# Score matmuls in fours, x scaled in one VectorE pass, and another order of the seven products

## The chip, the cores and the metric

The kernel runs on one core of a Trainium2 chip. Its engines are TensorE (PE in the profile; PEld are its weight loads), VectorE (DVE), ScalarE (ACT), GpSimd (POOL) and SyncE (SP, which here issues most of the DMA transfers). Each engine works through its own queue in order, and semaphores tie the queues together. The metric is the device time of one execution in microseconds (us); lower is better. The kernel before took 2226.36 us, the median of 3 runs (2225.69 to 2230.63).

## What is computed

One layer of a streaming encoder, for a prompt of 512 tokens and for 8 running streams with 16 new tokens each, 640 tokens in all, of width 2048. One input projection feeds 6 stick-breaking heads, 6 band heads and 4 memory heads of width 128, their gates, and three merge gates of width 2048:

```python
def rms_norm(x, g):
    xf = x.astype(jnp.float32)
    xf = xf * lax.rsqrt(jnp.mean(xf * xf, axis=-1, keepdims=True) + RMS_EPS)
    return (xf * g.astype(jnp.float32)).astype(x.dtype)

def stick_breaking(q, k, v, q_pos, k_pos):
    z = jnp.einsum('bqhd,bkhd->bhqk', q, k).astype(jnp.float32) * (HEAD_DIM ** -0.5)
    ...

def merge_output(x, o_sb, g_sb, o_bd, g_bd, o_mm, g_mm, mg_sb, mg_bd, mg_mm,
                 w_up_sb, w_up_band, w_up_mem, w_out, g_post):
    ...
    merged = (jax.nn.sigmoid(mg_sb) * branch(o_sb, g_sb, w_up_sb)
              + jax.nn.sigmoid(mg_bd) * branch(o_bd, g_bd, w_up_band)
              + jax.nn.sigmoid(mg_mm) * branch(o_mm, g_mm, w_up_mem))
    return x + rms_norm(merged @ w_out, g_post)
```

Three places matter here. `rms_norm(x, g_pre)` is applied to x before the projection. The scores q·k of the sample tokens against the cached keys of each stream (512 keys, 256 in the memory heads) stand in all three kinds of attention. The merge gates are sigmoids of the columns of `rms_norm(x) @ w_in` that belong to them.

## The kernel before

**Numbers and tiles.** Activations lie transposed, channels on the 128 partitions and the 640 tokens in two halves of 320 (`HF`). A projection multiplies in three matmuls: each weight and each activation is split into a high and a low part (`split`, L96 on ACT for the high part, L97 on DVE for the low), and high by high, high by low and low by high are added up (`mm3`, L148 to L150, and `proj`, L162). Weights come in pieces: SP loads a tile `wr`, ACT and DVE make `wh` and `wl` of it, 128x512 at a time, with four buffers each, and PE uses them.

**Stages.** From 0 to 97 us the keys and values of the memory tokens are projected (L148 to L150 into `acc`), and woven into that the five tiles of x are loaded, normalised, transposed on PE and split (`norm_x`, L232 to L249): ACT sums the squares (L185), DVE works out the scale (`rms_scale`, L131 to L137, on 128x1 tiles `rs`), POOL multiplies by the gain `gbx` (L237), DVE by the scale (L238), PE transposes (L243). Until 985 us follow the twelve causal heads, alternately stick-breaking and band; until 1190 us the four memory heads and the first four gates; until about 1742 us the other 44 gates as 22 pairs; then the upward projections and the output projection with its norm.

**A head.** Four projections give gate, value, query and key. Then `interleave` takes turns between the attention of the prompt and `sample_att`. The latter handles the eight streams in two rounds (`par` 0 and 1) of four. For each stream, DVE transposes cached keys `kc` into a tile `kt` (L486, four buffers); then four matmuls (L490) multiply 32 columns of `qm` each by one `kt` and write 32 partitions each of the score tile `s`, at column position 32·j of the array.

**A pair of gates.** `gate_pair` computes two column blocks by two halves of the tokens with seven products in place of eight. Each `product` is 24 matmuls (L687) into one of three banks `qa`, `qb`, `qc`; products on `qa` accumulate through the pair, and after some of them the bank is copied (ACT) or added (DVE, L697) into the output tiles `o0`, `o1`, on which ACT then applies the sigmoid. The weight sums s1 to s4 are made on POOL.

**Order.** The code is written with tiles and dependencies; a scheduler of the tile framework sets, when the program is built, the order of every engine's queue, by a timeline of its own. `tc.issue_after` limits where an instruction may stand in the queue and adds no wait.

Of the kernel before, what the change touches and what calls it, by code (L numbers as in the profile page):

```python
# [11 lines left out]
ALU = mybir.AluOpType  # L12
# [31 lines left out]
def stream_step_kernel(  # L44
# [8 lines left out]
    PE, ACT, DVE, POOL, SP = nc.tensor, nc.scalar, nc.vector, nc.gpsimd, nc.sync  # L53
# [122 lines left out]
    with ExitStack() as m0:  # L176
# [27 lines left out]
        for k0 in range(0, KB, 2):  # L204
            tp = bank("tp").rearrange("p (k n) -> p k n", k=2)
            for kk in range(2):
                k = k0 + kk
                for t in range(2):
# [4 lines left out]
                                         op0=ALU.mult, op1=ALU.subtract)  # L213
# [11 lines left out]
        gbx = pm.tile([P, D], F32, name="gbx")  # L225
# [6 lines left out]
        def norm_x(t):  # L232
            xr = raw_rows()
            for v, src in blocks(xr, x_p, x_s, t):
                SP.dma_start(v, src)
            r = rms_scale(sumsq(xr), pm, "rs0")
            POOL.tensor_tensor(xr, xr, gbx, op=ALU.mult)  # L237
            DVE.tensor_scalar(xr, xr, r, None, op0=ALU.mult)  # L238
            for kg in range(4):
                tp = bank("tp")  # L240
                for i in range(4):
                    k = kg * 4 + i
                    PE.transpose(tp[:, i * P:(i + 1) * P], xr[:, k * P:(k + 1) * P], ident)  # L243
                tv = tp.rearrange("p (i n) -> p i n", i=4)
                for j in range(2):
                    a, b = max(t * P, j * HF), min((t + 1) * P, (j + 1) * HF)
                    if a < b:
                        h, l = (xq[kg // 2][j][n][:, kg % 2 * 4:kg % 2 * 4 + 4, a - j * HF:b - j * HF] for n in range(2))
                        split(h, l, tv[:, :, a - t * P:b - t * P])  # L249
# [48 lines left out]
    def ext_ap(h, off, dims):  # L298
        t = rext_d[h:h + 1, off:off + 1]
        return bass.AP(tensor=t.tensor, offset=t.offset, ap=dims)  # L300

    def interleave(*gens):
        gens = list(gens)
# [156 lines left out]
    def sample_att(ck, cv, qr, kr, vn, sg, kind, strips):  # L460
        nkb = ck.shape[1] // P
        nc_ = nkb * P
        new = kind != "mm"
        vcs = {}

        def load_v(b):
            t = pa.tile([P, nkb, P], F32, tag="vc", name="vc", bufs=B["vc"])
            SP.dma_start(t, cv[b].rearrange("(k p) e -> p k e", p=P))
            return t

        def load_k(b):

            t = pa.tile([P, 2 * nc_ // 32, 32], F32, tag="kc", name="kc", bufs=B["kc"])
            for a in range(4):
                SP.dma_start(t[32 * a:32 * a + 32],
                             ck[b:b + 2, :, 32 * a:32 * a + 32].rearrange("b (c j) i -> j (b c) i", j=32))
            return t.rearrange("p c i -> p (c i)")

        s = bank("s")
        for par in range(2):  # L480
            kts = []
            for j in range(0, 4, 2):
                kc = load_k(4 * par + j)
                for h in range(2):
                    kt = pa.tile([P, nc_], F32, tag="kt", name="kt", bufs=B["kt"])
                    DVE.transpose(kt, kc[:, h * nc_:(h + 1) * nc_])  # L486
                    kts.append(kt)
                    yield
            for j in range(4):
                PE.matmul(s[32 * j:32 * j + 32, :nc_], qm[:, j, par * 32:par * 32 + 32], kts[j],  # L490
                          start=par == 0, stop=par == 1, tile_position=(0, 32 * j))
            yield
        b = pa.tile([P, NT if new else nc_], F32, tag="b", name="b", bufs=B["b"])
        if new:
            s2 = bank("s2")
            PE.matmul(s2[:, :P], qr, kr, start=True, stop=True)
        if kind == "sb":
            e = pa.tile([P, NT], F32, tag="e", name="e", bufs=B["e"])
            for src, c in ((s, slice(0, TP)), (s2[:, :P], slice(TP, NT))):
                ACT.activation(b[:, c], src, AF.Sigmoid, scale=SCALE)  # L500
                ACT.activation(e[:, c], src, AF.Sigmoid, scale=-SCALE)
            POOL.tensor_tensor(b[:, TP:], b[:, TP:], msb, op=ALU.mult)
            DVE.tensor_tensor(e[:, TP:], e[:, TP:], nsb, op=ALU.max)
            stick(b, e, NT)
        elif kind == "bd":
            for src, c, st in ((s, slice(0, TP), strips[0]), (s2[:, :P], slice(TP, NT), strips[1])):
                DVE.scalar_tensor_tensor(b[:, c], src, SCALE, st[:, ::-1], op0=ALU.mult, op1=ALU.add)
            softmax(b, b)
        else:
            softmax(b[:, :nc_], s[:, :nc_], SCALE)  # L510
        yield
        for b_ in range(NB):
            vcs[b_] = load_v(b_)
        tp = bank("tp")
        for kb in range(nkb):
            PE.transpose(tp[:, kb * P:(kb + 1) * P], b[:, kb * P:(kb + 1) * P], ident)
        ACT.copy(masked(wTm, nkb), tp[:, :nc_].rearrange("p (j a i) -> p j a i", a=2, i=TS))
        o = bank("o")
        if new:
            t2 = bank("t2")  # L520
            PE.transpose(t2[:, :P], b[:, TP:], ident)
            wn = pa.tile([P, P], F32, tag="wn", name="wn")
            DVE.tensor_copy(wn, t2[:, :P])
        yield
        steps = [(par, kb) for par in range(2) for kb in range(nkb)]
        if new:
            steps = ["new"] + steps
        for i, st in enumerate(steps):
            for j in range(4):
                if st == "new":  # L530
                    l, r = wn[:, 32 * j:32 * j + 32], vn
                else:
                    par, kb = st
                    l, r = wTm[:, kb, j, par * 32:par * 32 + 32], vcs[4 * par + j][:, kb]
                PE.matmul(o[32 * j:32 * j + 32, :P], l, r, start=i == 0, stop=i == len(steps) - 1,  # L535
                          tile_position=(0, 32 * j))
        on = pa.tile([P, P], F32, tag="on", name="on")
        ACT.copy(on, o[:, :P])
        yield
        t3 = bank("t3")  # L540
        PE.transpose(t3[:, :P], on, ident)
        DVE.tensor_tensor(sg[:, TP:], t3[:, :P], sg[:, TP:], op=ALU.mult)
# [58 lines left out]
    with tc.tile_pool(name="att", bufs=1, reuse_waits="tile") as pa:  # L601
        qm, wTm = zero_padded(4)
# [40 lines left out]
    with tc.tile_pool(name="attm", bufs=1, reuse_waits="tile") as pa:  # L643
        qm, wTm = zero_padded(2)
# [7 lines left out]
    t3, t4 = b12, operand(4, tpool2)  # L652
# [21 lines left out]
    def gate_pair(i):  # L674
        (a11, a12), (a21, a22) = load_quads(C_GATE + i * P)

        def comb(eng, a, b, op):
            t = sw.tile([P, KH, P], F32, tag="ws", name="ws", bufs=3)
            for c, o in enumerate(pieces(t)):
                eng.tensor_tensor(o, a[c], b[c], op=op)  # L680
            return pieces(t)

        def product(bank_, w, x, first):
            wh, wl = parts_of(w)
            for k in range(KH):
                for n, (a, b) in enumerate(((wh, x[0]), (wh, x[1]), (wl, x[0]))):
                    PE.matmul(bank_, a[:, k], b[:, k], start=first and k == 0 and n == 0, stop=k == KH - 1 and n == 2,  # L687
                              skip_group_check=not first)

        def half():  # L690
            return bank("q")[:, :HF]

        o0, o1 = (stg.tile([P, NT], F32, tag="sig", name="sig") for _ in range(2))
        lo, hi = slice(0, HF), slice(HF, NT)

        def add(t, q):
            DVE.tensor_tensor(t, t, q, op=ALU.add)  # L697

        s1 = comb(POOL, a21, a22, ALU.add)
        s2 = comb(POOL, s1, a11, ALU.subtract)  # L700
        s3 = comb(POOL, a11, a21, ALU.subtract)
        qa, qb = half(), half()
        product(qa, a11, b11, True)
        ACT.copy(o0[:, lo], qa)
        product(qb, a12, b21, True)
        add(o0[:, lo], qb)
        product(qa, s2, t2, False)
        ACT.copy(o0[:, hi], qa)
        qc = half()
        product(qc, s1, t1, True)  # L710
        ACT.copy(o1[:, hi], qc)
        s4 = s2
        for a, b in zip(a12, s2):
            POOL.tensor_tensor(b, a, b, op=ALU.subtract)
        product(qc, s4, b22, False)
        add(o0[:, hi], qc)
        product(qa, s3, t3, False)
        add(o1[:, hi], qa)
        ACT.activation(o0, o0, AF.Sigmoid)
        put_sig(i, o0)  # L720
        product(qa, a22, t4, False)
        ACT.activation(o1[:, hi], o1[:, hi], AF.Sigmoid)
        ACT.activation(o1[:, lo], qa, AF.Sigmoid)
        put_sig(i + 1, o1)
# [136 lines left out]
```

## Time and profile before

| | |
|---|---|
| median of 3 runs | 2226.36 us (2225.69 to 2230.63) |
| profiled execution | 2225.07 us |
| its span in the profile | 2223.4 us, 36183 instructions |
| granted TensorE clock, mean | 0.984 |
| HBM read, written | 249.97 MB, 36.19 MB |
| DMA packets | 574006, 288.55 MB |

The profile shows one execution. In its rows, `out<-in` names the tiles written and read, `L490` is a line of the kernel, and `x8` says that eight instructions of one form stand together in a row. A timeline row gives start and duration in us and, in brackets, how long the engine stood idle before it and for whom. A group row gives the durations' minimum, median and maximum in ns. A window row gives, for a stretch of time, its length and each engine's busy time and instruction count, then the granted TensorE clock as a share of full speed, the DMA engines' busy share and their GB/s. Matmuls are pipelined: a row's duration is longer than the distance to the next row's start.

### The profile page before, as it was taken

The page shows a single profiled execution, that of the slowest core. Times are in us where ns is not written, and L with a number is a line of the kernel's source. Part 1 is how long each engine was busy: PE and PEld are TensorE (multiplying, and loading weights), DVE is VectorE, ACT ScalarE, POOL GpSimd, SP SyncE. Part 2 cuts the span into 40 slices and gives each one's busy share as a digit, 9 for nine tenths or more (in the row PEclk, how much of TensorE's full clock was granted, in tenths as well). Part 3 has the DMA queues.
Part 4 walks back from the last instruction along what each step waited for, and adds up shares of the span by engine and source line. Part 5 has one row for each costly group of instructions (what it writes and reads, how often), then busy time and mean ns, then how long its engine had stood idle before and what let it go on. Part 6 is the DMA issues. An engine that isn't in the chain of part 4 may idle for free.

```text
span 2223.4 us, 36183 instructions
## 1 busy us (share of the span) xinstructions
PE 2147.6 (97%) x14277; PEld 1992.9 (90%) x14277; DVE 1074.8 (48%) x1795; ACT 789.0 (35%) x1484; POOL 423.1 (19%) x443
## 2 busy tenths in 40 slices
PE   6999999999999999999997999999999999999997
PEld 4899899898988999978986999999999899998886
DVE  7624444444444444438438555555555434582224
ACT  6422333333323333224344444444444312232221
POOL 3100010000100100000003444544544002340000
PEclk8999999999999999999999999999999999999998
DMA  7665556555564646525442433343333545443224
GB/s 232 181 152 117 133 130 150 128 129 138 146 148 99 155 130 151 144 71 132 124 109 71 132 117 100 104 131 115 100 107 113 161 143 167 145 152 110 76 85 161
DMA packets 574006, 288.55 MB, mean 130 GB/s; under 512 B 277488, under 2 KB 537600, under 8 KB 572812
## 3 DMA queue, kind: packets, MB, share of 16 engines
q1 hardware_dynamic: 560748, 253.18, 43.1%
q10 hardware_dynamic: 9216, 19.93, 2.3%
q0 software_dynamic: 3872, 13.13, 1.7%
q8 instruction: 112, 1.84, 0.3%
q14 instruction: 58, 0.48, 0.1%
HBM read 249.97 MB, written 36.19 MB: 129 GB/s over the span
## 4 chain that ended last, share of the span: by engine, by line
PE 75%; issue 13%; DVE 5%; DMA 3%; POOL 2%; SPq 1%; ACT 1%; ACTq 0%; DVEq 0%; POOLq 0%
PE acc L162 33%; PE q L687 23%; PE ya L148 3%; PE ya L150 3%; PE ya L149 3%; PE s L490 3%; DVE wl L97 2%; POOL merged L764 1%; PE o L535 1%; DMA sig<-sig_d 1%; DMA st<-rext_d 1%; PE tp L413 1%; PE acc L149 0%; PE o L149 0%; DVE yt L828 0%
## 5 line engine op out<-in xcount | busy, mean ns | idle before, releaser
L97 DVE TENSOR_TENSOR wl<-wr,wh 128x512 fp32r<-128x512 f32 (+1 forms) x548 | 411.2, 753 | 621.6 <-ACT wh L96 618.6
L96 ACT CAST wh<-wr 128x512 fp32r<-128x512 f32 (+1 forms) x548 | 330.5, 607 | 806.8 <-PE acc L162 463.6
L162 PE MATMUL acc<-xl,wh 128*128 128x320 f32 x1920 | 453.7, 312 | 0.0
L162 PE MATMUL acc<-xh,wh 128*128 128x320 f32 x1920 | 447.5, 312 | 4.7 <-ACT sig L633 2.5
L162 PE MATMUL acc<-xh,wl 128*128 128x320 f32 x1920 | 450.5, 312 | 0.0
L162 PEld LDWEIGHTS acc<-xh,wh 128*128 128x128 f32 x1920 | 323.8, 189 | 25.0 <-issue 18.6
L162 PEld LDWEIGHTS acc<-xh,wl 128*128 128x128 f32 x1920 | 324.3, 189 | 18.0 <-issue 18.0
L162 PEld LDWEIGHTS acc<-xl,wh 128*128 128x128 f32 x1920 | 325.8, 189 | 15.4 <-issue 14.7
L687 PE MATMUL q<-xh,wh 128*128 128x320 f32 x704 | 218.3, 311 | 5.1 <-ACT wh L96 5.1
L97 DVE TENSOR_TENSOR wl<-ws,wh 128x512 fp32r<-128x512 f32 x176 | 154.6, 879 | 140.1 <-ACT wh L96 139.9
L687 PE MATMUL q<-xh,wl 128*128 128x320 f32 x704 | 214.8, 310 | 5.8 <-DVE wl L97 5.8
L687 PE MATMUL q<-xl,wh 128*128 128x320 f32 x704 | 218.0, 310 | 0.0
L687 PE MATMUL q<-th,wh 128*128 128x320 f32 x528 | 163.2, 309 | 0.7 <-DVE sig L697 0.7
L687 PE MATMUL q<-th,wl 128*128 128x320 f32 x528 | 163.2, 309 | 0.0
L687 PE MATMUL q<-tl,wh 128*128 128x320 f32 x528 | 163.1, 309 | 0.0
L96 ACT CAST wh<-ws 128x512 fp32r<-128x512 f32 x176 | 109.1, 621 | 151.8 <-PE q L687 151.8
L687 PEld LDWEIGHTS q<-xh,wh 128*128 128x128 f32 x704 | 133.1, 189 | 5.6 <-ACT wh L96 5.6
L687 PEld LDWEIGHTS q<-xh,wl 128*128 128x128 f32 x704 | 132.0, 189 | 6.7 <-DVE wl L97 6.7
L687 PEld LDWEIGHTS q<-xl,wh 128*128 128x128 f32 x704 | 133.1, 189 | 0.0
L148 PE MATMUL ya<-wh,gh 128*128 128x512 f32 x320 | 126.6, 396 | 1.0 <-DVE sig L763 1.0
L150 PE MATMUL ya<-wh,gl 128*128 128x512 f32 x320 | 126.6, 395 | 0.0
L149 PE MATMUL ya<-wl,gh 128*128 128x512 f32 x320 | 126.6, 395 | 0.0
(204 smaller groups left out, 3100.9 us busy)
## 6 DMA issues: line engine op xcount, KB each, us to landing
wr<-in_w_in_dram SPq DMA_DIRECT2D x208, 512.0 KB, 4.5
wr<-in_w_out_dram SPq DMA_DIRECT2D x32, 512.0 KB, 3.7
sig_d<-sig ACTq DMA_DIRECT2D x48, 320.0 KB, 3.4
sig<-sig_d SPq DMA_DIRECT2D x48, 320.0 KB, 3.4
kc<-in_cache_sb_k_dram SPq DMA_DIRECT2D x96, 128.0 KB, 3.2
vc<-in_cache_sb_v_dram SPq DMA_DIRECT2D x48, 256.0 KB, 5.8
kc<-in_cache_band_k_dram SPq DMA_DIRECT2D x96, 128.0 KB, 3.2
vc<-in_cache_band_v_dram SPq DMA_DIRECT2D x48, 256.0 KB, 5.1
```

The lines of the kernel that those rows point to most:

```text
L96: ACT.copy(hi, src)
L97: DVE.tensor_tensor(lo, src, hi.bitcast(F32), op=ALU.subtract)
L148: PE.matmul(out, ah, bh, start=start, stop=False)
L149: PE.matmul(out, ah, bl, start=False, stop=False)
L150: PE.matmul(out, al, bh, start=False, stop=stop)
L162: PE.matmul(acc[:, s, :HF], a[:, k], b[s], start=first and f, stop=last and l)
L413: PE.transpose(tp[:, kb * P:(kb + 1) * P], b[:, kb * P:(kb + 1) * P], ident)
L490: PE.matmul(s[32 * j:32 * j + 32, :nc_], qm[:, j, par * 32:par * 32 + 32], kts[j], start=par == 0, stop=par == 1, tile_position=(0, 32 * j))
L535: PE.matmul(o[32 * j:32 * j + 32, :P], l, r, start=i == 0, stop=i == len(steps) - 1, tile_position=(0, 32 * j))
L687: PE.matmul(bank_, a[:, k], b[:, k], start=first and k == 0 and n == 0, stop=k == KH - 1 and n == 2, skip_group_check=not first)
L764: POOL.tensor_tensor(merged[:, j], merged[:, j], sig, op=ALU.add)
```

## The change

Three edits. In `norm_x` the multiplication by the gain on POOL and the one by the scale on DVE become one instruction on DVE. In `sample_att` the matmul of stream 3 of a round is issued first, and the other three are kept in the queue after it, so that a round's four matmuls depend on the same moment. In `gate_pair` the product of s3 and its addition stand ahead of the product of s4 and its addition.

```diff
@@ norm_x
-            POOL.tensor_tensor(xr, xr, gbx, op=ALU.mult)
-            DVE.tensor_scalar(xr, xr, r, None, op0=ALU.mult)
+            DVE.scalar_tensor_tensor(xr, xr, r, gbx, op0=ALU.mult, op1=ALU.mult)
@@
+    def ins_of(x):
+        return x.ins if hasattr(x, "ins") else x
@@ sample_att
-            for j in range(4):
-                PE.matmul(s[32 * j:32 * j + 32, :nc_], qm[:, j, par * 32:par * 32 + 32], kts[j],
-                          start=par == 0, stop=par == 1, tile_position=(0, 32 * j))
+            def score(j):
+                return PE.matmul(s[32 * j:32 * j + 32, :nc_], qm[:, j, par * 32:par * 32 + 32], kts[j],
+                                 start=par == 0, stop=par == 1, tile_position=(0, 32 * j))
+
+
+            with tc.issue_after(ins_of(score(3))):
+                for j in range(3):
+                    score(j)
@@ gate_pair
+        product(qa, s3, t3, False)
+        add(o1[:, hi], qa)
         product(qc, s4, b22, False)
         add(o0[:, hi], qc)
-        product(qa, s3, t3, False)
-        add(o1[:, hi], qa)
         ACT.activation(o0, o0, AF.Sigmoid)
```

What the scheduler made of it, in three places. The first is PE's queue in the first stick-breaking head, the second round of scores (`s` is the score tile, `acc` the projection of the next head's gate). Before:

```order
L490 MATMUL s_1425<-kt_1512,qm_883 32x512
L162 MATMUL acc_1790<-xh10_77,wl_1852 128x320
L162 MATMUL acc_1790<-xh11_79,wl_1852 128x320
L162 MATMUL acc_1790<-xh10_77,wh_1851 128x320
L162 MATMUL acc_1790<-xh11_79,wh_1851 128x320
L490 MATMUL s_1425<-kt_1519,qm_883 32x512
L162 MATMUL acc_1790<-xl10_78,wh_1851 128x320
L162 MATMUL acc_1790<-xl11_80,wh_1851 128x320
L162 MATMUL acc_1790<-xh10_77,wl_1852 128x320
L162 MATMUL acc_1790<-xh11_79,wl_1852 128x320
L490 MATMUL s_1425<-kt_1540,qm_883 32x512
```

Of the change:

```order
L162 MATMUL acc_1785<-xl10_78,wh_1846 128x320
L492 MATMUL s_1420<-kt_1541,qm_878 32x512
L492 MATMUL s_1420<-kt_1507,qm_878 32x512
L492 MATMUL s_1420<-kt_1514,qm_878 32x512
L492 MATMUL s_1420<-kt_1535,qm_878 32x512
L162 MATMUL acc_1785<-xl11_80,wh_1846 128x320
```

The four stand together now, close to where the fourth single one stood. In all second rounds of the twelve causal heads it is so, and in those of three memory heads; in the fourth memory head the four stand as two and two. The first rounds stand as before.

The second place is DVE's queue at the first tile of x (`rs` is its scale, `xr` the tile, `ml`, `wl` and `xl` are low parts). Before:

```order
L137 TENSOR_TENSOR rs_438<-rs_438 128x1
L212 SCALAR_TENSOR_TENSOR ml<-tp,gT,mh 128x256
L97 TENSOR_TENSOR wl<-wr,wh 128x512 x2
L238 TENSOR_SCALAR xr<-xr,rs_438 128x2048
L97 TENSOR_TENSOR wl<-wr,wh 128x512 x2
L131 TENSOR_SCALAR rs_503<-ss 128x1
```

Of the change:

```order
L137 TENSOR_TENSOR rs_438<-rs_438 128x1
L237 SCALAR_TENSOR_TENSOR xr<-xr,rs_438,gbx 128x2048
L212 SCALAR_TENSOR_TENSOR ml<-tp,gT,mh 128x256
L97 TENSOR_TENSOR wl<-wr,wh 128x512 x4
L131 TENSOR_SCALAR rs_502<-ss 128x1
```

The scaling moved up by three instructions, right behind the scale that it needs; in POOL's queue only the five rows of L237 are gone.

The third place is ACT's queue at the end of a gate pair (`ws` are the weight sums, `wr` and `wr2` loaded weights, the last casts those of the next pair; `sig` are o0 and o1). Before:

```order
L96 CAST wh_12897<-ws_12724 128x512
L96 CAST wh_12901<-ws_12724 128x512
L711 COPY sig_12717<-q_12828 128x320
L96 CAST wh_12932<-wr_12712 128x512
L96 CAST wh_12936<-wr2_12714 128x512
L96 CAST wh_12988<-wr_12967 128x512
L719 ACTIVATE sig_12716<-sig_12716 128x640
L96 CAST wh_12992<-wr2_12969 128x512
```

Of the change:

```order
L96 CAST wh_12892<-ws_12716 128x512
L96 CAST wh_12896<-ws_12716 128x512
L718 COPY sig_12712<-q_12823 128x320
L96 CAST wh_12927<-wr_12707 128x512
L96 CAST wh_12931<-wr2_12709 128x512
L729 ACTIVATE sig_12712<-sig_12712 128x320
L96 CAST wh_12983<-wr_12962 128x512
L96 CAST wh_12987<-wr2_12964 128x512
L726 ACTIVATE sig_12711<-sig_12711 128x640
```

The sigmoid of o0 (128x640) stood between the two casts of the next pair's first product and now stands behind both; that of half of o1 (128x320) moved up ahead of them. On PE the two moved products now stand one after the other, 24 matmuls each, where they were interleaved with each other before.

## Prediction, on record before the change was run

> **What bounds the kernel now.** I read the page from the top: busy shares, the slices of the span, the chain that ended last.
>
> ```profile
> PE 2147.6 (97%) x14277; PEld 1992.9 (90%) x14277; DVE 1074.8 (48%) x1795; ACT 789.0 (35%) x1484; POOL 423.1 (19%) x443
> PE   6999999999999999999997999999999999999997
> PE acc L162 33%; PE q L687 23%; PE ya L148 3%; PE ya L150 3%; PE ya L149 3%; PE s L490 3%; DVE wl L97 2%; POOL merged L764 1%; PE o L535 1%; DMA sig<-sig_d 1%; DMA st<-rext_d 1%; PE tp L413 1%; PE acc L149 0%; PE o L149 0%; DVE yt L828 0%
> ```
>
> TensorE is busy for 97% of the span; only the first slice and two others fall below nine tenths. The chain runs along PE, and the score matmuls (s, L490) hold 3% of it, about 67 us. Which engine sets the pace must be read stage by stage, so I then took the windows of three stages: start, causal heads, gate pairs.
>
> ```profile
> core 0: us, PE busy (x) PEld busy (x) DVE busy (x) ACT busy (x) POOL busy (x), PEclk, DMA share, GB/s
> 24.00:45.00 21.00, 10.23 (x39) 7.61 (x38) 20.05 (x20) 7.79 (x13) 14.36 (x4) 0.76 0.45 163
> 45.00:70.00 25.00, 19.41 (x104) 16.14 (x103) 23.12 (x32) 16.00 (x30) 11.17 (x4) 0.96 0.64 152
> 180.00:985.00 805.00, 805.00 (x5867) 731.41 (x5865) 349.53 (x627) 255.48 (x498) 60.65 (x180) 1.00 0.56 134
> 1240.00:1700.00 460.00, 460.00 (x3138) 460.00 (x3137) 245.18 (x318) 209.21 (x373) 214.52 (x148) 1.00 0.35 114
> ```
>
> In the causal heads PE is busy for all 805 us, in the gate pairs for all 460; nothing else is near full there (DVE 349.53 of 805, DMA 0.56). So in those stages only PE time counts. In the start PE works 10.23 of 21 us while DVE is full, 20.05 of 21: there DVE counts. The change touches all three stages.
>
> **The scores in fours.** The timeline of PE shows both forms already. A sample head issues two rounds of four score matmuls, each 32 columns wide in a column group of its own. In a stick-breaking head round one stands together, round two as four single ones between projection matmuls. The trace counts every score matmul as two ("x2"), so x8 is a whole round.
>
> ```profile
> 182.63 0.28 PE L148 MATMUL o<-wth,vh 128*128 128x256 f32 x1
> 182.84 1.07 PE L490 MATMUL s<-kt,qm 128*32 128x512 f32 x8
> 183.84 0.39 PE L149 MATMUL o<-wtl,vh 128*128 128x256 f32 x1
> 184.06 0.28 PE L150 MATMUL o<-wth,vl 128*128 128x256 f32 x1
> 184.18 0.29 PE L148 MATMUL o<-wth,vh 128*128 128x256 f32 x1
> ...
> 186.65 0.46 PE L162 MATMUL acc<-xh,wh 128*128 128x320 f32 x2
> 186.94 0.46 PE L162 MATMUL acc<-xl,wh 128*128 128x320 f32 x2
> 187.33 1.05 PE L490 MATMUL s<-kt,qm 128*32 128x512 f32 x2
> 188.31 0.56 PE L162 MATMUL acc<-xh,wl 128*128 128x320 f32 x2
> 188.70 0.46 PE L162 MATMUL acc<-xh,wh 128*128 128x320 f32 x2
> ```
>
> PE is pipelined, so I price by starts, not by durations. Undisturbed, two 320-column matmuls start every 0.29 us (186.65 to 186.94), 0.147 each; 256 columns take 0.12 (184.06 to 184.18). From 186.94 to 188.70 are 1.76 us with four 320-column matmuls in them, 0.59: one single score costs 1.17 us. From 182.63 to 184.06 are 1.43 us with two 256-column matmuls, 0.24: four scores together cost 1.19 us. Four cost what one costs. In the change's order every second round of the twelve causal heads stands as four; before, all twelve stood as singles. Saved: 12 × (4 × 1.17 − 1.19) = 12 × 3.49 = **42 us**. The memory heads have 256 columns:
>
> ```profile
> 1022.37 0.64 PE L490 MATMUL s<-kt,qm 128*32 128x256 f32 x8
> 1022.94 0.41 PE L162 MATMUL acc<-xh,wl 128*128 128x320 f32 x1
> 1023.19 0.45 PE L162 MATMUL acc<-xh,wh 128*128 128x320 f32 x2
> ...
> 1027.10 0.62 PE L490 MATMUL s<-kt,qm 128*32 128x256 f32 x2
> 1027.64 0.41 PE L162 MATMUL acc<-xl,wh 128*128 128x320 f32 x1
> 1027.99 0.62 PE L490 MATMUL s<-kt,qm 128*32 128x256 f32 x2
> ```
>
> The single one takes 0.54 us to the next start and lengthens its neighbours by 0.20 (0.35 − 0.147 from 1027.64 to 1027.99), 0.74 in all; the four take 0.57 and the same 0.2, 0.77. Sixteen singles cost 12 us; in the new order three heads have a four and one has two pairs, 3 × 0.77 + 2 × 0.74 = 3.8. Saved: **8 us**, with bounds of 6 (part of it lost behind the waits at the stage's end) and 10 (some singles cost more).
>
> A group must wait for its last key tile, the singles wait each for their own. So I looked when the transposes that make the tiles run:
>
> ```profile
> 183.93 2.49 DVE L486 STREAM_TRANSPOSE kt<-kc 128x512 f32<-128x512 f32 x4 [3.26 <-PE s L490]
> ```
>
> All four tiles of the round that starts at 187.33 are done at 186.42, before even the first single. The group stands close to where the fourth single stood, so it adds no wait; the four tile buffers come free up to three or four us later, but round two has no successor in its head, and the next head fills them after its own projections. PE being full, what is cut from it is cut from the end. Bounds of the 42: none of it is hidden, as PE has no idle time in this stage; a quarter, 10 us, could go if DVE or the loads, at 43% and 0.56 of a stage that shrinks by 5%, came late in places.
>
> Here one rule of the notes speaks against the change. The Trainium skill, "TensorE: Matmul & The Clock Gate", section "Part 3: Packing small matmuls — row/col tiling", says that a weight load runs beside matmuls in flight only where its row group differs; these four use all rows and differ in their columns alone. By the row of x8 above, 1.07 us against 1.05 for x2, the trace does not agree for this form; by the rule the sum below would be 20 us in place of 66 (rival 3).
>
> **x scaled in one DVE pass.** Before, each of five x tiles takes a multiplication on POOL (L237) and one on DVE (L238).
>
> ```profile
> L237 POOL TENSOR_TENSOR xr<-xr,gbx x5: 4500/4572/4642, 24.0 to 61.9; 128x2048 f32<-128x2048 f32 x5
> 24.63 4.58 DVE L97 TENSOR_TENSOR wl<-wr,wh 128x512 fp32r<-128x512 f32 x1 [0.51 <-ACT wh L96]
> 30.62 9.60 DVE L137 TENSOR_TENSOR rs<-rs 128x1 f32<-128x1 f32 x1
> 51.79 6.44 DVE L97 TENSOR_TENSOR wl<-wr,wh 128x512 fp32r<-128x512 f32 x4
> 61.91 5.60 DVE L238 TENSOR_SCALAR xr<-xr,rs 128x2048 f32<-128x2048 f32 x1
> ```
>
> DVE's rows are long wherever POOL works: a tensor_tensor over one element per partition lasts 9.60 us, as long as two POOL passes. Against their usual lengths (0.68, 0.15, four at 0.6, 1.28) these rows hold 3.9 + 9.4 + 4.0 + 4.3 = 21.6 us in which DVE was held up. The change removes all five POOL passes. What PE loses by it:
>
> ```profile
> 41.27 0.80 PE L149 MATMUL acc<-wl,mh 128*128 128x512 f32 x1 [10.33 <-DVE wl L97]
> 44.37 0.40 PE L150 MATMUL acc<-wh,ml 128*128 128x512 f32 x1
> 44.61 0.40 PE L148 MATMUL acc<-wh,mh 128*128 128x512 f32 x1
> 56.48 0.49 PE L149 MATMUL acc<-wl,mh 128*128 128x512 f32 x1 [1.67 <-DVE wl L97]
> 67.65 3.15 PE L243 MATMUL tp<-ident,xr 128*128 128x128 f32 x16 [3.91 <-DVE xr L238]
> 80.86 1.91 PE L243 MATMUL tp<-ident,xr 128*128 128x128 f32 x16
> ```
>
> The waits are 10.33 + 1.67 + 3.91 = 15.9 us. After a long one PE also runs slower for a while: seven starts from 41.27 take 3.1 us where 0.24 each would make 1.7, and the transposes at 67.65 take 1.2 longer than those at 80.86. That is 2.6 more, 18.5 in all. Against this stands a new load on DVE. The scalar_tensor_tensor over 2048 elements isn't in the trace; its kind is:
>
> ```profile
> L828 DVE SCALAR_TENSOR_TENSOR yt<-yt,rs,xres x20: 743/746/753, 2190.9 to 2218.9; 128x512 f32<-128x512 f32 x20
> L212 DVE SCALAR_TENSOR_TENSOR ml<-tp,gT,mh x16: 473/476/484, 6.7 to 40.1; 128x256 fp32r<-128x256 f32 x16
> ```
>
> From 256 to 512 elements it grows by 0.27 us, so 1536 more cost 1.62: 2.36 us. Bounds: 1.28, the median of the pass that it replaces (the row at 61.91 less its 4.3), and 4 × 0.746 = 2.98. So DVE gets 5 × 1.08 = 5.4 us more. From 24 to 70 its own work is 43.2 − 21.6 = 21.6; with 5.4 it is 27 in about 30 us, so it is nearly full and the added time shows in part: I take half, 2.7, back. Gain: 18.5 − 2.7 = 15.8, with **16 us** as value. Bounds: 8, where only the longest wait goes and DVE's new work shows whole (10.33 + 2.6 − 5.4 = 7.5), and 19, where nothing comes back.
>
> **The order of the products.** PE is full in the gate pairs already, so a better order has nothing to win: 0 from above. From below, in the new order ACT's Sigmoid of o0 stands between casts of the next pair's weights, and would hold them up if o0 came late. What covers it is ACT's lead, seen in the waits of that stage:
>
> ```profile
> ACT wh L96 <- PE q L687: 257.5, 244, 1.4
> ```
>
> The casts wait 244 times for PE to free a buffer: ACT is ahead by its four buffers, two products, 2 × 24 × 0.147 = 7 us. The sum that Sigmoid waits for ends two products before the one whose casts stand behind it. I take **0**, and 5 us either way for what the stage ends do.
>
> **Sum.** 42 + 8 + 16 + 0 = 66 us. The profiled execution took 2225.07 us (span 2223.4); 2225.07 − 66 = 2159; its time is 1.3 under the median, 2226.36, which gives 2160.4. **Forecast: 2160 us.**
>
> **Rivals.** (1) *The start gives less.* DVE is nearly full there; if it is late for x's tiles too, or the loads of x are what PE waits for next, 8 to 0 of the 16 us remain: 2168 to 2176. For it: DVE busy 20.05 of 21. Against: two thirds of that (3.9 + 9.4) is POOL's hold. (2) *The group waits for its tiles.* If the fourth tile is late by 2 us in each of 16 rounds, 32 us go: 2192. For it: the transposes of before waited for PE to free tiles (3.26 in the row above). Against: they end 0.9 us before the first single. (3) *The four do not overlap in the new places.* Then a group of four still spares the lengthening of neighbours three times, 0.6 us, and shows three weight loads of 0.11 that were covered:
>
> ```profile
> L490 PEld LDWEIGHTS s<-kt,qm x256: 106/108/109, 182.8 to 1172.0; 128*32 128x32 f32 x128
> ```
>
> That is 16 × (0.6 − 0.33) = 4 us, and with the start's 16 it makes 2205. The change would not do what it says. The x8 rows speak against it. The rule of the Trainium skill cited above would give this time. (4) *Slower: the gate pairs turn on ACT.* Sigmoid of o0 waits for the last of the two moved products, casts queue behind it, PE runs dry once a pair. There are 22 pairs, so from 66 / 22 = 3.0 us a pair on it eats everything; with 3.5 us, one product's length (24 × 0.147), 77 us go: 2237. Against: the lead of 7 us. (5) *More than forecast*: DVE keeps up at the start and the memory heads' waits shrink: below 2150.
>
> **How the numbers follow.** Forecast 0.72; rival 1 0.10, 2 0.07, 3 0.04, 4 0.04, 5 0.03. The low end takes the upper bounds, 42 + 10 + 19 + 5 = 76: 2150, opened to 2148. The high end takes the lower bounds, 8 from the start, 6 from the memory heads, 32 from the causal heads: 46, so 2180. Cases 1 and the forecast lie inside, with 0.82. What a measurement can tell from no change is 0.2%, 4.5 us: faster 0.94, same 0.02, slower 0.04. Slower is rival 4; same is the part of rival 2 in which other losses meet it.
>
> **What would show it.** Right: rows of s x8 with about 1.07 us in every second round, PE busy in all of the causal stage and the stage 42 us shorter; no L237 on POOL; no DVE row of one element per partition above 0.2 us at the start; the 10.33 gone; L237 on DVE at 2.4 us; gate pairs still wholly busy. Wrong: waits of s for kt, x8 rows of 4 us, idle PE before q, or PE waiting on xr or wl between 24 and 70 for over 8 us.

## The result, and the profile after

The changed kernel took 2160.41 us, the median of 4 runs (2158.63 to 2161.72), against 2226.03 (4 runs, 2223.01 to 2230.63) of the kernel before: a ratio of 0.9703, with a 95% interval from 0.9685 to 0.9721, 66 us less. The forecast was 2160. Its profiled execution took 2158.63 us with a span of 2156.8. The head of its page, busy shares and two rows of the slices:

```profile
PE 2092.2 (97%) x14277; PEld 1980.1 (92%) x14277; DVE 1060.2 (49%) x1795; ACT 791.6 (37%) x1484; POOL 402.2 (19%) x438
PE   7999999999999999989989999999999899999997
```

TensorE's count is the same and its busy time 55 us less. The windows of the three stages, moved to where they stand now (columns as before):

```profile
24.00:45.00 21.00, 19.52 (x103) 15.74 (x101) 15.36 (x31) 13.45 (x23) 0.72 (x1) 1.00 0.95 234
45.00:70.00 25.00, 21.58 (x99) 16.47 (x98) 19.69 (x42) 17.46 (x37) 1.53 (x2) 0.93 0.64 195
165.00:928.00 763.00, 763.00 (x5867) 727.29 (x5869) 348.70 (x627) 256.64 (x499) 62.36 (x180) 1.00 0.59 141
1176.00:1636.00 460.00, 460.00 (x3139) 460.00 (x3138) 247.93 (x318) 210.61 (x375) 214.74 (x149) 1.00 0.35 115
```

The causal window holds the same 5867 matmuls in 763 us instead of 805, and PE is still busy for all of it. The gate pairs are full as before. In the start PE works 19.52 us of 21 instead of 10.23, DVE has fallen from 20.05 to 15.36, and a new number stands out: the DMA engines are busy for 0.95 of that window, where they were at 0.45.

To see where the 66 us come from I read the starts of the same matmuls in the traces of the kernel before, the changed kernel and the three kernels with one edit each (below). Lengths in us:

| stage | before | changed | scores alone | x pass alone | products alone |
|---|---|---|---|---|---|
| to the first score | 182.8 | 168.0 | 183.2 | 168.6 | 185.1 |
| first to last causal score | 801.6 | 760.2 | 760.2 | 801.6 | 801.6 |
| to the first product of the gate pairs | 205.2 | 197.0 | 197.1 | 204.3 | 205.1 |
| first gate pair | 38.8 | 36.2 | 41.6 | 39.0 | 37.5 |
| other gate pairs | 518.2 | 517.3 | 518.2 | 518.2 | 517.3 |
| to the last matmul's end | 462.8 | 463.5 | 462.8 | 462.5 | 464.4 |

The changed kernel gains 14.8 us in the start (forecast 16), 41.4 in the causal heads (42), 8.2 in the memory heads (8), 2.6 in the first gate pair and 0.2 in what follows it; 0.6 us came back behind the last matmul. The timeline of PE in the second round of the first head shows what carries it:

```profile
173.60 0.46 PE L162 MATMUL acc<-xh,wh 128*128 128x320 f32 x2
173.89 0.31 PE L162 MATMUL acc<-xl,wh 128*128 128x320 f32 x1
174.13 1.06 PE L492 MATMUL s<-kt,qm 128*32 128x512 f32 x8
175.13 0.41 PE L162 MATMUL acc<-xl,wh 128*128 128x320 f32 x1
175.38 0.45 PE L162 MATMUL acc<-xh,wl 128*128 128x320 f32 x2
```

From 173.89 to 175.38 are 1.49 us with two 320-column matmuls of 0.147: 1.19 us for the four scores, the price that the first rounds had before. No idle time stands ahead of the row: the group waits for no key tile.

### The profile page after: what moved, and what is told of

It reads as the page before. It is cut to its first block, busy times and chain, and to the rows that moved or that the text cites. A ratio compares the mean times of both kernels' runs of the same rounds, so it can differ in the third digit from the quotient of the medians.

```text
span 2156.8 us, 36248 instructions
## 1 busy us (share of the span) xinstructions
PE 2092.2 (97%) x14277; PEld 1980.1 (92%) x14277; DVE 1060.2 (49%) x1795; ACT 791.6 (37%) x1484; POOL 402.2 (19%) x438
## 2 busy tenths in 40 slices
DMA packets 574007, 288.55 MB, mean 134 GB/s; under 512 B 277488, under 2 KB 537600, under 8 KB 572812
## 4 chain that ended last, share of the span: by engine, by line
PE 76%; issue 12%; DMA 4%; DVE 3%; POOL 2%; SPq 1%; ACT 1%; ACTq 0%; DVEq 0%; POOLq 0%
PE acc L162 33%; PE q L694 25%; PE ya L148 3%; PE ya L150 3%; PE ya L149 3%; DVE wl L97 1%; PE s L492 1%; POOL merged L771 1%; PE o L542 1%; DMA sig<-sig_d 1%; DMA wr<-in_w_mem_kv_dram 1%; DMA st<-rext_d 1%; DMA or<-osg_d 1%; PE tp L415 1%; PE o L149 0%
## 5 line engine op out<-in xcount | busy, mean ns | idle before, releaser
L162 PE MATMUL acc<-xh,wh 128*128 128x320 f32 x1920 | 441.1, 310 | 4.9 <-ACT sig L640 2.5
L97 DVE TENSOR_TENSOR wl<-ws,wh 128x512 fp32r<-128x512 f32 x176 | 150.1, 853 | 143.1 <-ACT wh L96 142.4
```

What stands on the lines that cost most here:

```text
L97: DVE.tensor_tensor(lo, src, hi.bitcast(F32), op=ALU.subtract)
L162: PE.matmul(acc[:, s, :HF], a[:, k], b[s], start=first and f, stop=last and l)
```

## The experiments

Each is given with its own runs of the kernel before on the same chip; ratios are to those, with 95% intervals.

**One edit at a time.** Three kernels: the kernel before with the scores in fours, with the single DVE pass, and with the other order of the products, each edit taken from the diff above.

> The kernel before with the score matmuls in fours as the only edit. Theory (four cost what one costs, and PE is full): 42 us from the causal heads and 8 from the memory heads, the causal stage 805 to about 763 us, 2226 - 50 = 2176 us. Rival (the changed kernel's gain comes mostly from its start, and the groups only move waits): less than 25 us, above 2200.

> The kernel before with x scaled in one DVE pass as the only edit. Theory (POOL's passes hold DVE, DVE is the start's bound): the first projection of a head starts 13 to 16 us earlier, the rest is unchanged: 2211 us. Rival (the longer DVE pass gives it back): 2220 or more.

> The kernel before with the other order of the seven products as the only edit. Theory (PE is full in the gate pairs in both orders): no change, 2226 us within 3. Rival 1 (the first and the last pair, where PE is not full, shrink, as the 2.6 and 0.9 us between the two traces hint): 2222 to 2223. Rival 2 (casts queue behind the sigmoid): slower by 3 us a pair, above 2280.

Scores alone: 2180.3 us, ratio 0.9799 (0.9780 to 0.9818), 45 us less, where the theory had 50. The stages it touches gave what was expected: the causal heads 41.4 us and the memory heads 8.0. Of the missing 5 us the trace shows 3.2 where the edit changes nothing: the first gate pair was 2.8 us longer and the start 0.4. Another 2.1 us lie behind the last matmul. The rival fell. The x pass alone: 2211.61 us, 0.9943 (0.9925 to 0.9960), 13 us less, as expected; in its trace the first score is 14.3 us earlier and nothing else moved by more than 1 us. The products alone: 2222.53 us (12 runs), 0.9995 (0.9984 to 1.0007): no difference. Its trace has the shorter first pair (1.2 us) and other pairs (0.9), and a longer rest (1.6). The first score came 2.3 us later there and the end behind the last matmul was 2.3 us longer; the profiled execution is the longest of the twelve.

The three ratios add up to 58 us of gain, the whole change has 66; each of these has an interval of about 4 us either way. In the traces the scores' and the x pass's own stages add up without a rest, and the largest difference lies in the first gate pair, 41.6 us with the scores alone and 36.2 with all three edits. That pair stands right behind the stage's last waits, and differs from kernel to kernel, but the order of the products sorts it: in the traces of all kernels here it takes 36.2 to 37.6 us with the new order (eight kernels) and 38.8 to 41.6 with the old one (six). So the third edit is worth some 1 to 5 us in that pair, and the three gains do not simply add up; which wait it shortens stays open.

**POOL back in the start.** The changed kernel with a POOL pass whose result nobody reads:

```diff
             DVE.scalar_tensor_tensor(xr, xr, r, gbx, op0=ALU.mult, op1=ALU.mult)
+            POOL.tensor_tensor(dead, xr, gbx, op=ALU.mult)
```

> The changed kernel, and behind each scaling of x one POOL multiplication of the same size whose result nobody reads. Theory (POOL's pass holds DVE while it runs): long DVE rows come back in the start, as many as there are POOL passes, and 8 to 15 us of the start's gain go, about 2172 us. Rival (what POOL cost was its place in the chain of x, scale after gain): nothing comes back, 2160 us within 3, and no long DVE rows.

It took 2171.68 us, 0.9766 (0.9744 to 0.9787): of the change's 3% a part of 0.6% was gone, 14 us by the ratios and 11 by the medians, and in the trace the first score is 10.5 us later than in the changed kernel. The timelines of POOL, DVE and PE show how:

```profile
31.45 4.53 POOL L239 TENSOR_TENSOR dead<-xr,gbx 128x2048 f32<-128x2048 f32 x1 [2.10 <-DVE xr L238]
```

```profile
31.68 6.66 DVE L97 TENSOR_TENSOR wl<-wr,wh 128x512 fp32r<-128x512 f32 x4
```

```profile
36.59 0.50 PE L149 MATMUL acc<-wl,mh 128*128 128x512 f32 x1 [3.14 <-DVE wl L97]
```

Nobody reads the dead pass's result, and in the trace no load waits for a POOL pass; yet the four DVE instructions that meet it take 6.66 us, where four took 2.49 at 29.43 in the changed kernel, and PE waits for them. So most of the price of POOL's passes, 10.5 of 14.8 us, is there without any place in the chain of x: they held DVE. The rest was not separated. The Trainium skill, "SBUF — State Buffer", section "Who interferes with whom", says that a DVE instruction with two SBUF inputs contends with a GpSimd instruction that reads SBUF, and that the ports which they share are an exclusive lock; these rows agree, with 4.2 us of hold by a pass of 4.53.

**Two DVE passes instead of one.** Is it the fusing or POOL's absence that pays? The first try moved the multiplication by the gain to DVE where it stood:

```diff
-            POOL.tensor_tensor(xr, xr, gbx, op=ALU.mult)
+            DVE.tensor_tensor(xr, xr, gbx, op=ALU.mult)
             DVE.tensor_scalar(xr, xr, r, None, op0=ALU.mult)
```

> The kernel before with the multiplication by the gain moved from POOL to DVE, so that x takes two DVE passes and no POOL pass. Theory (the gain comes from POOL's absence, not from the fusing): DVE has 5 x 2.4 us more than before but is not held for 21.6; 8 to 13 us faster than before, about 2215 us. Rival (the gain comes from one pass in place of two): no faster than before, 2224 us or more.

It took 2220.82 us, 0.9977 (0.9967 to 0.9988): 5 us less by the ratio, 3 by the medians, neither forecast. The trace shows where the gain went, in rows of DVE, PE and ACT:

```profile
59.38 2.29 DVE L237 TENSOR_TENSOR xr<-xr,gbx 128x2048 f32<-128x2048 f32 x1 [9.35 <-ACT junk L185]
```

```profile
61.85 0.80 PE L148 MATMUL acc<-wh,mh 128*128 128x512 f32 x1 [8.25 <-ACT wh L96]
```

```profile
57.34 1.91 ACT L185 ACTIVATE junk<-xr 128x2048 f32<-128x2048 f32 x1 [10.69 <-DMA xr<-in_x_sample_dram]
61.15 0.65 ACT L96 CAST wh<-wr 128x512 fp32r<-128x512 f32 x1
```

The scheduler put the last tile's multiplication into DVE's queue ahead of other work. There it stood for 9.35 us, until ACT had read the tile (`junk`). But PE's 8.25 us ended with a cast of ACT, and that cast stood in ACT's own queue behind the square sum of the same tile, which waited 10.69 us for the tile's load. So both queues stood for one late load. The expectation of the next kernel blames DVE's queue alone; by these rows that is not what ended PE's wait. What made the load late in this build was not separated. The next kernel exchanged the two passes, so that both stand behind the scale:

> The kernel before with x multiplied on DVE in two passes, first by the scale and then by the gain, so that both stand behind the scale. The experiment with the gain first gained only 3 us, with DVE waiting 9.35 us in its queue for the load and the square sum of the last x tile. Theory (that wait is what ate its gain, and POOL's absence is what counts): no such wait, five passes of 2.3 more than in the changed kernel less 1.1 each, 6 us more DVE work of which half shows: 10 us faster than before, 2214 us. Rival (the fusing is what counts): 2220 us or more.

2224.06 us, 0.9995 (0.9986 to 1.0004): no gain at all, and my expectation missed a second time. But its first projection started 13.1 us earlier than before (ACT's wait for that load was 2.9 us, and no multiplication stood long in DVE's queue). The gain was there and went before the first score, which came 1.1 us earlier. POOL's timeline and PE's row:

```profile
131.55 0.75 POOL L567 TENSOR_SCALAR_AFFINE_SELECT st<-st 128x128 f32<-128x128 f32 x2 [13.81 <-DMA st<-rext_d]
132.25 0.29 POOL L329 COPY vnT<-vt 128x128 f32<-128x128 f32 x1
```

```profile
132.59 0.48 PE L332 MATMUL t<-ident,vnT 128*128 128x128 f32 x1 [11.39 <-POOL vnT L329]
```

In this build the scheduler had put a band head's strip instruction (`st`), which waits 13.81 us for a load, ahead of the small copy `vnT`, for which PE waits. The last kernel changed that order alone:

```diff
-        POOL.tensor_copy(ns.rearrange("p (a j i) -> p a j i", a=2, i=TS), stream_order(src[:, TP:]))
+        copies.append(ins_of(POOL.tensor_copy(ns.rearrange("p (a j i) -> p a j i", a=2, i=TS), stream_order(src[:, TP:]))))
...
-            for base, cm, step in ((TS - P, 1, TS), (P - 1, -1, -TS)):
-                POOL.affine_select(st3, st3, pattern=[[step, NB], [0, TS]], compare_op=ALU.is_ge,
-                                   fill=NEG, base=base, channel_multiplier=cm)
+            with tc.issue_after(copies[-1]):
+                for base, cm, step in ((TS - P, 1, TS), (P - 1, -1, -TS)):
+                    POOL.affine_select(st3, st3, pattern=[[step, NB], [0, TS]], compare_op=ALU.is_ge,
+                                       fill=NEG, base=base, channel_multiplier=cm)
...
```

> The kernel before with x in two late DVE passes, and POOL's instructions on the band strips (st) queued behind the copy of the same pair's new keys. The experiment with two late passes reached the first projection 13.1 us earlier than before, but the first score only 1.1 us earlier: PE waited 11.39 us for a copy (vnT) that stood in POOL's queue behind strip instructions that waited for their load. Theory (POOL's absence from the start is what counts, not the fusing, and that queue order gave it back): the waits of PE for vnT and for knT (4.6 us in the kernel before) both go, 13 + 4 = 17 us faster than before, 2208 us. Rival (two passes are worth nothing against the fused one for another reason): 2220 us or more.

2209.02 us, 0.9928 (0.9906 to 0.9950), as expected. The wait for `vnT` fell to 0.2 us, that for `knT` is gone, and the first score came 15.4 us earlier than before. Part of this is the order on POOL, which also took away a wait for `knT` that the kernel before has (4.6 us). The first projection, ahead of all that, came 12.8 us earlier, against 12.2 with the fused pass alone. So two passes on DVE, without POOL, are worth in the start what the one is; the rival fell.

**How many stand together.** The changed kernel with a round tied in twos:

```diff
-            with tc.issue_after(ins_of(score(3))):
-                for j in range(3):
-                    score(j)
+            for j in (1, 3):
+                with tc.issue_after(ins_of(score(j))):
+                    score(j - 1)
```

> The changed kernel with the four score matmuls of a round tied in twos instead of fours. Theory (a group costs what one costs, whatever its size): each second round costs 2 x 1.175 in place of 1.19, 12 x 1.16 = 14 us more in the causal heads and 3 x 0.75 = 2 in the memory heads, 2176 us. Rival (the gain lies in the tie to the last tile, that is in when the scores run, not in how many stand together): 2160 us.

2179.61 us, 0.9791 (0.9770 to 0.9811). From its first to its last causal score are 773.7 us against 760.2 in the changed kernel: 13.5 for twelve rounds, 1.13 a round where 1.16 was expected. The memory heads are 3.3 us longer; the start (2.6) and the first gate pair (1.0) make up the rest. In its timeline a pair costs what a single one costs, 1.18 us (177.07 to 178.84 less four matmuls of 0.147):

```profile
177.07 0.46 PE L162 MATMUL acc<-xh,wl 128*128 128x320 f32 x2
177.46 1.05 PE L492 MATMUL s<-kt,qm 128*32 128x512 f32 x4
178.44 0.56 PE L162 MATMUL acc<-xh,wh 128*128 128x320 f32 x2
178.84 0.46 PE L162 MATMUL acc<-xl,wh 128*128 128x320 f32 x2
```

**All rounds in fours.** With a scheduling priority all 32 rounds stand as fours, in the band heads' first rounds too:

```diff
-            with tc.issue_after(ins_of(score(3))):
+            with tc.high_priority(), tc.issue_after(ins_of(score(3))):
```

> The changed kernel with the scores given priority in the scheduler, so that all 32 rounds stand as fours: also the first rounds of the six band heads and the memory head's that stand as two and two. Theory: 6 x 1.16 = 7 us and 0.75 less, 2152.5 us. Rival (the group that moves ahead waits for its last key tile, since the first rounds' tiles are made just before their use): 2160 us or more, with PE idle before s.

2153.83 us, 0.9681 (0.9664 to 0.9698). The causal heads went from 760.2 to 752.3 us, 7.8 where 7 was expected; the start was 1.4 us later than the changed kernel's. Its ratio lies below that of the changed kernel by 0.2%, with intervals that overlap: the trace shows the gain of the stage, the runs alone don't settle it.

**What sets the price of a group.** The groups can be made larger, by repeating matmuls of the first rounds:

> As the one with all rounds in fours, but in each first round every score matmul is issued twice, the two of one column group behind each other (3 3 0 0 1 1 2 2). The first of the two results is overwritten by the same numbers. Theory (matmuls run side by side only in different column groups, in the order of issue): about five times 0.97 and 0.2 a round, 5.1 us in place of 1.19; 12 x 3.9 + 4 x 2.2 = 55 us more than with all rounds in fours. Rival (the price is that of a switch between matmul forms, and neighbours of one form are cheap): under 10 us more.

> As the one with all rounds in fours, but in each first round the score matmul of column group 3 is issued four times and the others once (3 0 1 2 3 3 3), seven in all; all but the last result of group 3 are overwritten by the same numbers. Before it, doubling all four (3 3 0 0 1 1 2 2) cost 11.1 us, and its row shows sixteen records in 1.95 us. Theory (each column group works through its own matmuls, side by side with the others): the longest column counts, 4 x 0.9 us: a row of 3.6 us in the stick-breaking heads, 12 x 2.65 + 4 x 1.4 = 37 us more than with all rounds in fours. Rival (a fixed price for each neighbour of the same form, 0.24 us): 7 x 0.24 = 1.7 us, 8 us more.

The edit gives the order of issue of a round (the second kernel has `[3, 0, 1, 2, 3, 3, 3]`):

```diff
+                order = [3, 3, 0, 0, 1, 1, 2, 2] if par == 0 else [3, 0, 1, 2]
```

Doubled, 2164.93 us (2 runs), 0.9729 (0.9700 to 0.9759), 11.1 more than with all rounds in fours: the theory's 55 missed by far, and the rival's bound of 10 nearly held. Skewed, 2192.48 us (2 runs), 0.9849 (0.9827 to 0.9871) against 0.9681: 37 us more by the ratios, 39 by the medians, as the theory had it and far from the rival's 8. The first round of the first head, in the timelines of both:

```profile
167.49 1.95 PE L492 MATMUL s<-kt,qm 128*32 128x512 f32 x16
```

```profile
168.64 3.62 PE L492 MATMUL s<-kt,qm 128*32 128x512 f32 x14
```

Seven matmuls take longer than eight. Four on one column group cost 3.62 us, two on each of four groups 1.95. The longest column group sets the price, about 0.9 us for each matmul on it. What the first of these expectations had wrong was that PE would keep to the order of issue: a second matmul for a busy column group did not hold up those of other groups behind it. The rows do not name the column group, so this is read from the lengths, and from the starts: in the doubled order the first four matmuls start 14 ns apart, in the skewed one 7, as if every second one had been passed over.

**Loads in the start.** The kernel with all fours, and the x tiles spread:

```diff
-                      *((at, lambda t=t: norm_x(t)) for t, at in enumerate(range(6, 11)))):
+                      *((at, lambda t=t: norm_x(t)) for t, at in enumerate((5, 7, 9, 11, 13)))):
```

> The kernel with all rounds in fours, and the x tiles woven into the start at steps 5, 7, 9, 11, 13 instead of 6 to 10, so that in the load queue one weight tile moves ahead of x's third tile and two ahead of the sample tile. Theory (after the change the start waits for its loads, DMA share 0.95 from 24 to 45 us): the wait of ACT for a weight tile (5.28 us in the changed kernel) shrinks and the first projection of a head starts 1 to 3 us earlier, 2151 us. Rival (the transfers are full whatever their order): no change within 2 us, and the wait moves to x.

2155.66 us, 0.9684 (0.9671 to 0.9698) against 0.9681: no change. In the list of waits from 24 to 75 us ACT's longest wait now stands ahead of a square sum of x (`junk`), and PE waits 9.9 us for casts, 4.1 in the kernel with all fours:

```profile
PE acc L148 <- ACT wh L96: 9.9, 2, 5.7
ACT junk L185 <- DMA wr<-in_w_mem_kv_dram: 6.1, 1, 6.1
```

The second row names a weight tile, but this is the square sum of x's last tile, and it reads `xr` alone: it starts at 47.90 us, and the last of that tile's loads seen in the trace landed at 47.72. So the wait moved to x, as the rival had it. The order of the loads moved the wait and did not shorten it; that is what full transfers would do, but fewer bytes were not tried.

## Why the prediction was right, and where its reasons were not

**Scores, 42 us forecast, 41.4 measured.** Price and mechanism were right. 1.17 for one and 1.19 for four held in the new places, PE stayed full, no group waited for its tile (rival 2), and the twos and the skewed groups showed that the column groups really work side by side (rival 3 fell, and with it, for this form, the rule of the Trainium skill that the prediction cites: four in 1.06 us). That the saving is not hidden anywhere was argued from PE's full window, and the stage shrank by that sum in both kernels that have the edit.

**Memory heads, 8 forecast, 8.2 measured.** The first to the last score there came 6.4 us closer, less than the 8 that the prices gave, and the rest, 1.8 us, came between the last score and the first gate pair. The agreement is in part luck.

**x in one pass, 16 forecast, 14.8 in the changed kernel, 14.3 alone.** That POOL held DVE, and that this was the start's price, was right in the main; the dead pass and the two late passes show it from both sides. Of the 14.8 us 13.5 lie ahead of the first projection of a head, the stage that the forecast was about, and 1.3 behind it. The estimate of 2.36 us for the new pass was right too:

```profile
L237 DVE SCALAR_TENSOR_TENSOR xr<-xr,rs,gbx x5: 2348/2350/2352, 26.8 to 72.9; 128x2048 f32<-128x2048 f32 x5
```

Wrong was the step that gave 2.7 us back. It said that DVE would be nearly full and its added time show. DVE is busy for 15.36 of 21 us; what came back has another cause, in the waits from 24 to 70 us, and in rows of ACT and PE:

```profile
ACT wh L96 <- DMA wr<-in_w_mem_kv_dram: 9.6, 5, 5.3
PE acc L148 <- ACT wh L96: 3.3, 3, 1.6
```

```profile
46.31 1.14 ACT L96 CAST wh<-wr 128x512 fp32r<-128x512 f32 x2 [5.28 <-DMA wr<-in_w_mem_kv_dram]
```

```profile
46.98 0.50 PE L148 MATMUL acc<-wh,mh 128*128 128x512 f32 x1 [1.60 <-ACT wh L96]
```

A start that runs faster asks for its loads earlier, and the DMA engines, at 0.45 before, reach 0.95. The waits that PE has between 24 and 70 us now sum to 4.9 (seven of them, 0.23 to 1.60). Rival 1 named the loads, of x, as what PE might wait for next; it was a weight tile, asked for at 32.17 us among the loads of x's last tile and landed at 46.21, and it cost little. The size was near by luck: a term for one engine stood in for another's.

**Products, 0 forecast.** The edit alone changed nothing that 12 runs can tell (0.9984 to 1.0007), and the full windows are full in both orders. The first pair, where PE is not full (168 matmuls of 0.147 us make 24.7 of its 36 to 42), is shorter with it in every trace. In the changed kernel the casts still wait for PE's buffers, so ACT keeps its lead and rival 4 did not occur:

```profile
ACT wh L96 <- PE q L694: 255.3, 265, 1.4
```

The first pair's 2.6 us were not forecast. They lie within the 5 us that were allowed for the stage ends. That the total came out within 1 us of the forecast is luck in part: these 2.6 us made up for x's missing 1.2 and the 0.6 behind the last matmul.

## What to carry to other kernels

Price small matmuls from the starts of their neighbours, and look whether the trace has the grouped form already: here four in four column groups cost 1.19 us and one cost 1.17, so a tie in the queue order was worth 42 us on a full TensorE. When an engine shows long rows for small instructions, see what its neighbour runs at that moment: POOL passes that nobody waited for cost over 10 us. And when an edit frees time early in a program whose order a scheduler sets, follow it stage by stage: twice here 8 to 11 us came back as a wait in an in-order queue of the new schedule, once on ACT and DVE behind a load, once on POOL, and the total alone would have blamed the edit. A wait's named releaser is inferred: look which tile the waiting instruction reads before you believe it.

## What was not expected of the hardware

TensorE does not keep matmuls of different column groups in the order of issue: eight issued as 3 3 0 0 1 1 2 2 took 1.95 us, two lengths of about 0.9, where strict order makes five. What is said ahead of the prediction, that each engine works through its queue in order, does not hold for these. And a window's DMA share can double, from 0.45 to 0.95, while its rate grows by less than half, 163 to 234 GB/s, and the program moves the same 288.55 MB: loads that had been spread out now stand together, and a weight tile issued in that window takes 9.1 us to land at the median where it took 4.0.
